# Nearest-neighbour upsampling: one SBUF tile, output rows of up to 64 KB, 16 DMAs instead of 24

## Chip, cores and metric

The kernel runs on one core of one Trainium2 chip. The metric is device time in microseconds (us). Times are medians of several runs. The span is the time from the first to the last instruction in a profiled run; it is about 1.8 us shorter than the time.

A number called "landing" is the moment at which the last of a DMA's 16 completion writes arrives. Landings and packet durations are read from the trace's completion and packet records. Sizes of single loads, stores and rows are in binary units, as the profile gives them (a 4 MB store is 4096 KB); totals such as 83.89 MB and rates in GB/s are decimal.

## The reference

```python
x: (16, 64, 64, 64) float32, scale_factor = 2
result[:, :, i, j] = x[:, :, i // 2, j // 2]        # (16, 64, 128, 128) float32
```

Nothing is computed: 16.78 MB come in, and each value goes out four times, 67.11 MB. Together they are 83.89 MB.

## The kernel before

All of the input fits in SBUF, the on-chip memory. Eight loads of 2 MB bring it in at once, 64 input rows (16 KB) to a partition each. Then 16 stages expand 32 input rows per partition into one of two buffers, VectorE (DVE) the first 18 rows and ScalarE (ACT) the other 14, and a 4 MB store takes the buffer away. One input row becomes 1 KB of output, so a partition's piece of a store is one contiguous row of 32 KB.

```python
blocks = [64, 64, 64, 64, 64, 64, 64, 64]
K = 32
KV = 18
xpool = ctx.enter_context(tc.tile_pool(name="xin", bufs=1))
upool = ctx.enter_context(tc.tile_pool(name="uexp", bufs=2))

loaded = []
first = 0
for n, k in enumerate(blocks):
    xt = xpool.tile([P, k, W], fdt, name=f"x{n}")
    nc.sync.dma_start(out=xt[:, :, :], in_=of_block(xf, first, k))
    ...
for xt, first, k in loaded:
    for r0 in range(0, k, K):
        u = upool.tile([P, K, s, W, s], fdt, name="u")
        nc.vector.tensor_copy(out=u[:, :KV], in_=expanded(xt[:, r0 : r0 + KV, :]))
        nc.scalar.copy(out=u[:, KV:], in_=expanded(xt[:, r0 + KV : r0 + K, :]))
        nc.sync.dma_start(out=of_block(of, first, k)[:, r0 : r0 + K, :], in_=u[:, :, :, :, :])
```

`begin_before_barrier` (cut here) moves the first load ahead of the start-up barrier. The change leaves it doing the same.

## Time and profile before

The time is 199.88 us (median of 6 runs, 199.73 to 200.25), the span 198.0 us.

These are lines of the page of the kernel before. The DMA row gives the mean busy share of the 16 DMA engines in tenths, for 40 equal slices of the span; the row below it gives what they moved.

```profile
span 198.0 us, 149 instructions
...
DMA  8999999999999999999999999999999999999995
...
DMA packets 3456, 83.89 MB, mean 424 GB/s; under 512 B 384, under 2 KB 384, under 8 KB 384
...
L83 ACT COPY u<-x 128x3584 f32<-128x3584 f32 x16 | 50.8, 3179 | 128.3 <-DMA out_dram<-u 122.5
L80 DVE COPY u<-x 128x4608 f32<-128x4608 f32 x16 | 40.9, 2560 | 139.7 <-DMA out_dram<-u 131.8
...
out_dram<-u SPq DMA_DIRECT2D x16, 4096.0 KB, 16.1
x<-in_x_dram SPq DMA_DIRECT2D x8, 2048.0 KB, 22.9
```

The DMA engines are full from the second slice to the last but one. The copies take 3.2 us (ACT) and 2.6 us (DVE), and both engines idle most of the time, waiting for a store to free a buffer. The packet count splits exactly: 384 completion writes (24 DMAs on 16 engines) and 3072 data packets, one for each contiguous row (8 × 128 of 16 KB, 16 × 128 of 32 KB).

The busy time of the engines in four stretches confirms the constant pace. The columns are the stretch, its length, the busy time of DVE, ACT and POOL with instruction counts, the clock, the DMA share and GB/s.

```profile
20.00:60.00 40.00, 2.56 (x1) 3.18 (x1) 0.00 (x0) 1.00 1.02 432
60.00:100.00 40.00, 10.24 (x4) 12.71 (x4) 0.00 (x0) 1.00 1.00 433
100.00:140.00 40.00, 11.01 (x5) 13.50 (x5) 0.00 (x0) 1.00 1.00 433
140.00:180.00 40.00, 11.51 (x5) 13.98 (x5) 0.00 (x0) 1.00 1.00 433
```

The chain of waits needs more care. Its columns are start, duration and what; a DMA piece runs from issue to landing.

```profile
0.00 7.82 DMA x<-in_x_dram
...
103.70 16.06 DMA out_dram<-u
...
119.86 3.19 ACT u L83
...
123.06 16.05 DMA out_dram<-u
...
142.42 16.09 DMA out_dram<-u
...
158.60 3.19 ACT u L83
```

One could read this as a serial loop of copy (3.2 us) and store (16.1 us), with the fixed cost of a DMA on the critical path. But the chain follows only every second store, because a stage waits for the buffer of two stages ago. Two stores land within 123.06 + 16.05 − (103.70 + 16.06) = 19.35 us, 9.68 us each. A store waits 6.4 us of its 16.05 us behind the one before it. Copy and fixed cost are hidden. Only what makes the engines take longer for their bytes can matter.

### The profile page before, as it was taken

How to read it: one execution, taken by the hardware profiler on the slowest of the kernel's cores; microseconds unless marked ns; L12 is line 12 of the kernel's file. 1: busy time of each engine (PE TensorE's matmuls, PEld its weight loads, DVE VectorE, ACT ScalarE, POOL GpSimd, SP SyncE). 2: the span in 40 equal slices, each digit the busy share in tenths (PEclk: the TensorE clock that was granted, in tenths of full speed). 3: DMA queues.
4: the chain of work that ended last, by engine and by line, in shares of the span. 5: the costliest groups of instructions: out<-in, count | busy, mean ns of one | idle time of the engine just before them, and what ended most of it. 6: DMA issues, size and time to landing. Idle time of an engine off the chain costs nothing.

```text
span 198.0 us, 149 instructions
## 1 busy us (share of the span) xinstructions
DVE 40.9 (21%) x16; ACT 52.0 (26%) x17; POOL 0.2 (0%) x4
## 2 busy tenths in 40 slices
DVE  0460000000405050505050505050505050504000
ACT  2480000000415150606060606060606060605000
POOL 0000000000000000000000000000000000000000
DMA  8999999999999999999999999999999999999995
GB/s 268 434 434 434 430 427 430 424 427 424 424 424 437 444 463 430 437 430 430 424 424 424 424 437 444 457 437 430 437 430 424 424 424 424 437 437 463 437 430 232
DMA packets 3456, 83.89 MB, mean 424 GB/s; under 512 B 384, under 2 KB 384, under 8 KB 384
## 3 DMA queue, kind: packets, MB, share of 16 engines
q1 hardware_dynamic: 3456, 83.89, 99.0%
HBM read 16.78 MB, written 67.11 MB: 424 GB/s over the span
## 4 chain that ended last, share of the span: by engine, by line
DMA 77%; ACT 14%; issue 0%; ACTq 0%
DMA out_dram<-u 73%; ACT u L83 14%; DMA x<-in_x_dram 4%; ACTq L83 0%
## 5 line engine op out<-in xcount | busy, mean ns | idle before, releaser
L83 ACT COPY u<-x 128x3584 f32<-128x3584 f32 x16 | 50.8, 3179 | 128.3 <-DMA out_dram<-u 122.5
L80 DVE COPY u<-x 128x4608 f32<-128x4608 f32 x16 | 40.9, 2560 | 139.7 <-DMA out_dram<-u 131.8
L83 ACT ACT_TABLE_LOAD x1 | 1.3, 1283 | 0.8 <-PEq L106 0.8
L106 POOL MEMSET const-bfloat16-1.0<- 128x1 bf16 x1 | 0.1, 102 | 0.0
L106 POOL MEMSET const-uint8-127<- 128x1 uint8 x1 | 0.1, 102 | 0.0
L106 POOL MEMSET const-float32-0.0<- 128x1 f32 x1 | 0.1, 98 | 0.2 <-issue 0.2
L106 POOL MEMSET const-float32-1.0<- 128x1 f32 x1 | 0.1, 98 | 0.0
## 6 DMA issues: line engine op xcount, KB each, us to landing
out_dram<-u SPq DMA_DIRECT2D x16, 4096.0 KB, 16.1
x<-in_x_dram SPq DMA_DIRECT2D x8, 2048.0 KB, 22.9
```

Of the source, the lines that this page charges most:

```text
L80: nc.vector.tensor_copy(out=u[:, :KV], in_=expanded(xt[:, r0 : r0 + KV, :]))
L83: nc.scalar.copy(out=u[:, KV:], in_=expanded(xt[:, r0 + KV : r0 + K, :]))
L106: nc = _bacc.Bacc("TRN2", target_bir_lowering=False, num_devices=1)
```

## The change

The intent: fewer and longer pieces. One SBUF tile of 192 KB per partition holds the input (128 KB) and an output space (64 KB). The first half of the output leaves as before, through two halves of that space. By then half of the input is consumed, and the second half of the output leaves in four 8 MB stores whose pieces are rows of 64 KB. They alternate between the 64 KB of consumed input and the 64 KB of output space. The input comes in four loads of 4 MB; the fourth comes as four rows of 8 KB per partition. The 24 DMAs become 16.

```diff
-    blocks = [64, 64, 64, 64, 64, 64, 64, 64]
-    K = 32
-    KV = 18
+    WX = R // P * W
+    WU = 16384
+    mem_pool = ctx.enter_context(tc.tile_pool(name="mem", bufs=1))
+    mem = mem_pool.tile([P, WX + WU], fdt, name="mem")
+    M4 = R // (4 * P)
+    blocks = [(1, M4, 0), (1, M4, 2), (1, M4, 3), (4, M4 // 4, 1)]   # pieces, input rows in each, place
+    WB = M4 * W
 ... (the loads: one for each block, into mem[:, slot * WB : (slot + 1) * WB])
+    def store(part, r0, k, at):
+        xp, first, m = part
+        kv = k * 9 // 16
+        u = mem[:, at : at + k * s * W * s].rearrange(
+            "p (k a w b) -> p k a w b", k=k, a=s, w=W
+        )
+        nc.vector.tensor_copy(out=u[:, :kv], in_=expanded(xp[:, r0 : r0 + kv, :]))
+        nc.scalar.copy(out=u[:, kv:], in_=expanded(xp[:, r0 + kv : r0 + k, :]))
+        dst = of[first : first + P * m, :].rearrange("(p m) w -> p m w", p=P)
+        nc.sync.dma_start(out=dst[:, r0 : r0 + k, :], in_=u)
+    small = [(q, r0) for n in (0, 3) for q in parts[n] for r0 in range(0, q[2], 32)]
+    large = [(q, r0) for n in (1, 2) for q in parts[n] for r0 in range(0, q[2], 64)]
+    for n, (q, r0) in enumerate(small):
+        store(q, r0, 32, WX + n % 2 * (WU // 2))
+    for n, (q, r0) in enumerate(large):
+        store(q, r0, 64, (0, WX)[n % 2])
```

(The old loops, and a generalised `begin_before_barrier` that still moves one load, are cut.)

More of the change, by code (lines that the diff above doesn't have):

```diff
@@ L6 @@
 from concourse._compat import with_exitstack
+EARLY = 1
 def begin_before_barrier(nc):
@@ L15, in begin_before_barrier @@
     sp = mybir.EngineType.SP
-    load = next(i for i in body.instructions if i.engine == sp)
-    assert isinstance(load, mybir.InstDMACopy), type(load)
-    assert not (load.sync_info and load.sync_info.on_wait)
-    body.instructions = [i for i in body.instructions if i is not load]
+    loads = [i for i in body.instructions if i.engine == sp][:EARLY]
+    for load in loads:
+        assert isinstance(load, mybir.InstDMACopy), type(load)
+        assert not (load.sync_info and load.sync_info.on_wait)
+    names = [i.name for i in loads]
+    body.instructions = [i for i in body.instructions if i.name not in names]
     kept = list(main.instructions)
@@ L25, in begin_before_barrier @@
     )
-    kept.insert(at, load)
+    kept[at:at] = loads
     main.instructions = kept
@@ L44 @@
     fdt = x.dtype
-    blocks = [64, 64, 64, 64, 64, 64, 64, 64]
-    K = 32
-    assert P * sum(blocks) == R
-    KV = 18
+    WX = R // P * W
[5 more added lines that the diff above has]
+    WB = M4 * W
+    assert M4 * P * 4 == R and 2 * WB == WU
     xf = x.rearrange("b c h w -> (b c h) w")
     of = out.rearrange("b c (h hd) w -> (b c h) (hd w)", hd=s)
-    def of_block(rows, first, k):
-        return rows[first : first + P * k, :].rearrange("(p k) w -> p k w", p=P)
-    xpool = ctx.enter_context(tc.tile_pool(name="xin", bufs=1))
-    upool = ctx.enter_context(tc.tile_pool(name="uexp", bufs=2))
-    loaded = []
-    first = 0
-    for n, k in enumerate(blocks):
-        xt = xpool.tile([P, k, W], fdt, name=f"x{n}")
-        nc.sync.dma_start(out=xt[:, :, :], in_=of_block(xf, first, k))
-        loaded.append((xt, first, k))
-        first += P * k
+    parts = []
+    for n, (j, m, slot) in enumerate(blocks):
+        first = n * P * M4
+        xt = mem[:, slot * WB : (slot + 1) * WB].rearrange(
+            "p (j m w) -> p j m w", j=j, m=m
+        )
+        nc.sync.dma_start(
+            out=xt.rearrange("p j m w -> p j (m w)"),
+            in_=xf[first : first + P * M4, :].rearrange(
+                "(j p m) w -> p j (m w)", j=j, p=P
+            ),
+        )
+        parts.append([(xt[:, jj], first + jj * P * m, m) for jj in range(j)])
     def expanded(rows):
@@ L75, in expanded @@
         )
-    for xt, first, k in loaded:
-        for r0 in range(0, k, K):
-            u = upool.tile([P, K, s, W, s], fdt, name="u")
-            nc.vector.tensor_copy(
-                out=u[:, :KV], in_=expanded(xt[:, r0 : r0 + KV, :])
-            )
-            nc.scalar.copy(
-                out=u[:, KV:], in_=expanded(xt[:, r0 + KV : r0 + K, :])
-            )
-            nc.sync.dma_start(
-                out=of_block(of, first, k)[:, r0 : r0 + K, :],
-                in_=u[:, :, :, :, :],
-            )
+    def store(part, r0, k, at):
[3 more added lines that the diff above has]
+            "p (k a w b) -> p k a w b", k=k, a=s, w=W
+        )
+        nc.vector.tensor_copy(out=u[:, :kv], in_=expanded(xp[:, r0 : r0 + kv, :]))
[8 more added lines that the diff above has]
+        store(q, r0, 64, (0, WX)[n % 2])
 _INS = ['x', 'scale_factor']
```

## The prediction

> **What bounds the kernel now.** The DMA engines: 83.89 MB in a span of 198.0 us. The page's row of forty slices shows the DMA share full from the second slice to the last but one; the windows from 20 to 180 us show 432 to 433 GB/s each. The chain of waits gives ACT 14%, but misleads: stores take 16.05 us from issue to landing and land 9.68 us apart, so each is issued 6.4 us before its predecessor lands, and the 3.2 us copy is hidden. About 1.0 us passes before the first packet, 0.8 us after the last landing; 1.86 us lie between span and reported time.
>
> **What the change does.** Bytes and the DVE:ACT split (9:7) stay. 24 DMAs become 16: 8 loads of 2 MB become 3 of 4 MB in 32 KB rows and one of 4 MB in 8 KB rows; 16 stores of 4 MB become 8 the same and 4 of 8 MB in 64 KB rows. Data rows fall from 3072 to 2432 (192 to 152 per engine), completion writes from 384 to 256.
>
> **Cost of what is removed.** The tempting sum is 8 DMAs at the ~2 us fixed cost that the Trainium skill ("DMA: Bandwidth & Descriptors", Anatomy of one DMA) gives for a single DMA: 16 us. The trace denies it here: with another DMA queued, that latency is covered. What remains is a gap per row. Per engine, loads land 4.892 us apart for 8 rows of 16 KB, stores 9.680 us for 8 rows of 32 KB. If both directions run at one rate, that is 27.4 GB/s per engine and 0.104 us of overhead per DMA of 8 rows, some 12 ns per row. Estimate from this: three loads save 0.1 us each, the 8 KB-row load gives back 0.2, four large stores save 0.1 each: 0.5 us in all; 0.2 us if part of the loads' lower rate is due to direction. All of it is on the critical path.
>
> **What it adds, off the path.** A large store needs 5.1 us of DVE beside 6.4 us of ACT (twice today's). At today's pace, loads finish at 42 us and small stores land until 119.6. The first large store, over consumed input, is ready at 110, before the last small store streams. The second needs both small buffers free (119.6) and is ready at 126, while the first streams until 139; the others have 13 us of margin. The first copy waits for 4 MB (12.7 us instead of 7.8). The queue should never run dry.
>
> **Predicted: 199.4 us, 80% range 199.0 to 199.95.** Faster by over 2%: 1%; within 2%: 96%; slower by over 2%: 3%.
>
> **Right if:** DMA share full throughout; 4 MB stores still 9.68 us apart, large ones 19.26 rather than 19.36; 2432 data and 256 completion packets; DVE and ACT busy within 1 us; no gap.
>
> **Wrong if:** 64 KB rows are split in two packets (3200 instead of 2688; gain near 0.1 us); or the output pitch of 128 KB between partitions (64 KB before) slows HBM writes: the same page (Latency and other measured facts) reports 207 GB/s at a 512 KiB pitch against 214 at full rate; no run shows it yet; large stores over 19.5 us apart would. Or the start and the turn from loads to stores, which cost about 1 us and 0.25 us over the steady pace, change with the row size.

## The result, and the profile after

The time after is 199.50 us (median of 6, 199.42 to 199.63), against 199.88 us. The ratio is 0.998, with a 95% interval of 0.9967 to 0.9993. Ratios here are the mean time of one kernel's fast runs over that of the other's fast runs of the same rounds, so not quite the ratio of the medians. The gain is 0.1 to 0.7 us: about 0.2%, and inside the "within 2%" class. The span fell from 198.00 to 197.71 us.

Lines of the page after, to set beside those of before:

```profile
span 197.7 us, 116 instructions
...
DMA  8999999999999999999999999999999999999994
...
DMA packets 2688, 83.89 MB, mean 424 GB/s; under 512 B 256, under 2 KB 256, under 8 KB 256
...
L96 ACT COPY mem<-mem 128x3584 f32<-128x3584 f32 (+1 forms) x12 | 50.0, 4174 | 112.5 <-DMA out_dram<-mem 102.2
L95 DVE COPY mem<-mem 128x4608 f32<-128x4608 f32 (+1 forms) x12 | 40.2, 3359 | 123.1 <-DMA out_dram<-mem 110.8
...
out_dram<-mem SPq DMA_DIRECT2D x8, 4096.0 KB, 16.1
mem<-in_x_dram SPq DMA_DIRECT2D x4, 4096.0 KB, 25.8
out_dram<-mem SPq DMA_DIRECT2D x4, 32.3
```

The engines are as full as before, and the copies cost the same (50.0 against 50.8, 40.2 against 40.9 us). The 2688 packets are 256 completion writes and 2432 data packets; in the packet records 512 of them have 65,536 bytes, so a 64 KB row is one packet and is not split. An 8 MB store takes 32.3 us from issue to landing. That is no slowdown: it waits behind another 8 MB.

The stretches after, for the part where the load stage ends:

```profile
20.00:60.00 40.00, 2.56 (x1) 3.18 (x1) 0.00 (x0) 1.00 1.01 426
60.00:100.00 40.00, 15.20 (x5) 12.72 (x4) 0.00 (x0) 1.00 1.00 433
```

The stretch with the turn from loading to storing moves 426 GB/s where it moved 432. These figures are coarse where packets are large, but they point to the turn. The chain of waits after:

```profile
0.00 12.25 DMA mem<-in_x_dram
...
103.56 16.09 DMA out_dram<-mem
...
119.67 6.17 ACT mem L96
...
125.86 32.44 DMA out_dram<-mem
...
158.38 6.17 ACT mem L96
```

From 119.65 (103.56 + 16.09) to 158.30 (125.86 + 32.44) two large stores land, 38.65 us for 16 MB. Before, the same stretch, from 119.76 to 158.51, took four small stores 38.75 us. The larger ACT copy (6.17 us instead of 3.19) is hidden: the store issued at 125.86 still queues until the one ahead lands at 138.98.

The landings show where the gain came from. The five stages cover the same bytes in both kernels, and the times in us are worked out from the completion records of each profile. "Before again" is a second profile of the kernel before, from the experiments.

| stage | before | before again | after | after − before |
|---|---|---|---|---|
| first 4 MB in | 12.70 | 12.65 | 12.25 | −0.45 |
| next 8 MB in | 19.58 | 19.60 | 19.40 | −0.18 |
| last 4 MB in | 10.03 | 10.05 | 10.54 | +0.51 |
| first 32 MB out | 77.45 | 77.46 | 77.46 | +0.01 |
| last 32 MB out (64 KB rows after) | 77.43 | 77.43 | 77.25 | −0.18 |
| end, after the last landing | 0.81 | 0.81 | 0.81 | 0.00 |
| span | 198.00 | 197.99 | 197.71 | −0.29 |

The two profiles of before agree within 0.05 us in each stage, better than the times of repeated runs (0.3 us apart and more). Two profiles say little about the start and the turn, though. The two kernels of experiment 3 have the same loads as before, and there the first 4 MB took 12.78 and 12.57 us and the last 4 MB 10.46 and 10.37. Eight profiles whose first load is the same as in after spread from 12.16 to 12.41. The two store stages repeat far better (within 0.07 us wherever the stage and its rows are the same).

### The profile page after: what moved, and what is told of

Read it like the earlier page. It is cut to its first block, busy times and chain, and to the rows that moved or that the text cites. A ratio compares the mean times of both kernels' runs of the same rounds, so it can differ in the third digit from the quotient of the medians.

```text
span 197.7 us, 116 instructions
## 1 busy us (share of the span) xinstructions
DVE 40.2 (20%) x12; ACT 51.3 (26%) x13; POOL 0.2 (0%) x4
## 2 busy tenths in 40 slices
DMA packets 2688, 83.89 MB, mean 424 GB/s; under 512 B 256, under 2 KB 256, under 8 KB 256
## 3 DMA queue, kind: packets, MB, share of 16 engines
q1 hardware_dynamic: 2688, 83.89, 98.9%
## 4 chain that ended last, share of the span: by engine, by line
DMA 69%; ACT 14%; issue 0%; ACTq 0%
DMA out_dram<-mem 63%; ACT mem L96 14%; DMA mem<-in_x_dram 6%; ACTq L96 0%
## 5 line engine op out<-in xcount | busy, mean ns | idle before, releaser
L96 ACT COPY mem<-mem 128x3584 f32<-128x3584 f32 (+1 forms) x12 | 50.0, 4174 | 112.5 <-DMA out_dram<-mem 102.2
L95 DVE COPY mem<-mem 128x4608 f32<-128x4608 f32 (+1 forms) x12 | 40.2, 3359 | 123.1 <-DMA out_dram<-mem 110.8
## 6 DMA issues: line engine op xcount, KB each, us to landing
out_dram<-mem SPq DMA_DIRECT2D x4, 32.3
```

The lines of the kernel that those rows point to most:

```text
L95: nc.vector.tensor_copy(out=u[:, :kv], in_=expanded(xp[:, r0 : r0 + kv, :]))
L96: nc.scalar.copy(out=u[:, kv:], in_=expanded(xp[:, r0 + kv : r0 + k, :]))
```

## The experiments

Three theories were on the table:

- **Row theory.** Each contiguous row costs an engine a few ns beyond its bytes. The gain is proportional to the rows removed.
- **DMA theory.** Each DMA costs something, so the gain comes from 16 DMAs instead of 24.
- **For the load stage**, where a gain of 0.45 us at the start and a loss of 0.51 us at the end showed up: they follow the size of the rows, or the size of the DMAs.

In each experiment the kernel before ran in the same rounds on the same chip.

### 1. The 8 MB stores in 32 KB rows, still one DMA each

```diff
-        store(q, r0, 64, (0, WX)[n % 2])              # 64 rows of one part
+        # 32 rows of part 1 and 32 rows of part 2; their places in the output are not adjacent
+        nc.sync.dma_start(out=both[:, :, r0 : r0 + 32, :],
+                          in_=u.rearrange("p (n k) a w b -> p n k (a w b)", n=2))
```

The two expansions into one buffer take three copies instead of two; the copies stay hidden.

> The kernel after, but each 8 MB store writes two separate 32 KB rows per partition (32 rows of each of two parts), still one DMA: 64 more rows in all per 16 engines' worth of 8 rows, 16 DMAs as before. Row theory (a cost of about 6 to 9 ns per row and engine): the 8 MB stores land 19.36 us apart again instead of 19.31, the four together lose the 0.18 us that they gained, time 199.68. DMA theory (a cost per DMA): 19.31 us apart, time 199.5, because the number of DMAs is unchanged.

Measured: 199.74 us; ratio to before 0.9996 (0.9977 to 1.0015). The packets rose to 3200, as many as 64 KB rows split in two would give. Its chain of waits over the same two large stores:

```profile
103.69 16.07 DMA out_dram<-mem
...
125.97 32.50 DMA out_dram<-mem
```

From 119.76 to 158.47 these are 38.71 us, against 38.65. Over all four large stores, landings take 77.41 us: the pace of before (77.43), not of after (77.25). The DMA count did not change, so the DMA theory fails here.

### 2. The same rows, in twice as many DMAs

```diff
-        nc.sync.dma_start(out=dst[:, r0 : r0 + k, :], in_=u)
+        for h in range(0, k, 32):
+            nc.sync.dma_start(out=dst[:, r0 + h : r0 + h + 32, :], in_=u[:, h : h + 32])
```

> The kernel after, but each 8 MB store is issued as two 4 MB DMAs of 32 KB rows from the same buffer: 20 DMAs instead of 16. Row theory: pairs land 19.36 us apart as in the run with the same number of DMAs and two rows, plus 9 ns for a completion write, time 199.7. DMA theory: this one alone loses the gain, time 199.7, and the run with two rows per DMA does not. If DMAs cost near 2 us each[...], time is 207.

Measured: 200.15 us; ratio 1.0011 (0.9993 to 1.0029). The last 32 MB took 77.44 us, against 77.41 with half the DMAs: four more DMAs cost at most 0.03 us while the queue is full. The row theory had expected 199.7. The excess is not in the data stream at all: the last landing is at 197.10 us, yet the span ends at 198.16, so the end is 1.06 us instead of 0.81. The trace's records of SyncE explain it. At the end SyncE waits for the eight DMA semaphores, always in the same order, and the DMAs use them in turn. With 16, 24 or 72 DMAs the last DMA's semaphore is also the last waited for. With 20, four more waits follow it, about 62 ns each. Every run agrees: 0.81 us with 16, 24 and 72 DMAs, 1.06 with 20, 0.94 with 14 (two more waits). Part of this kernel's 200.15 us is so explained; the rest of the difference of its median is within the spread of its runs (199.92 to 200.34).

### 3. Stores in 8 KB rows, with 24 DMAs and with 72

To see a row's cost above the noise, the kernel before got rows four times shorter: 384 more rows for each engine. Once a store stays one DMA, once it is four.

```diff
+            dst = of_block(of, first, k).rearrange("p (j h i) w -> p j h i w", j=4, h=2)[:, :, h]
+            src = u.rearrange("p (j i) a w b -> p j i (a w b)", j=4)
-            nc.sync.dma_start(out=of_block(of, first, k)[:, r0 : r0 + K, :], in_=u[:, :, :, :, :])
+            nc.sync.dma_start(out=dst, in_=src)                     # b_rows8_same_dmas
+            for j in range(4):                                      # b_rows8_more_dmas
+                nc.sync.dma_start(out=dst[:, j], in_=src[:, j])
```

> The kernel before, but each 4 MB store writes four separate 8 KB rows per partition in one DMA instead of one row of 32 KB. The number of DMAs (24) stays; data rows rise by 384 per engine. Row theory: 384 times 6 to 9 ns, 2.3 to 3.5 us slower, stores land 9.83 to 9.90 us apart, time 202.2 to 203.4. DMA theory: no change, 199.9.

> The kernel before, but each 4 MB store is issued as four DMAs of 1 MB in 8 KB rows: 72 DMAs instead of 24, with the same 384 more rows per engine as the run with one DMA of four rows. Row theory: as that run plus 48 completion writes of 9 ns, 0.4 us: 202.6 to 203.8. DMA theory at the size that the gain of after suggests (0.38 us for 8 DMAs, 0.05 us each): 2.3 us slower, 202.2, while the run with one DMA stays at 199.9. At 2 us for each DMA: 296.

Measured: 203.59 us with 24 DMAs (ratio 1.0195, 1.0181 to 1.0209) and 203.17 us with 72 (1.0175, 1.0161 to 1.0189). The packet rows of the two pages, 24 DMAs first:

```profile
DMA packets 9601, 83.90 MB, mean 416 GB/s; under 512 B 384, under 2 KB 384, under 8 KB 384
```

```profile
DMA packets 10371, 83.92 MB, mean 417 GB/s; under 512 B 1152, under 2 KB 1152, under 8 KB 1152
```

Both kernels have 9216 data packets; the rest are completion writes and, by the packet records, one and three 8 KB packets of another queue, kind "instruction". Three times the DMAs made nothing slower; the kernel with more of them was even 0.4 us faster, for which no cause was sought. Against the 199.68 us of before on that chip, the shorter rows cost 3.9 and 3.5 us. The DMA theory asked for the opposite order and for no loss with 24 DMAs. The row theory has the direction right. Its size was somewhat low with 24 DMAs (2.3 to 3.5 us expected); with 72 (0.4 more expected) the time of 203.17 us lies inside its range.

The size is not one constant, though. With 24 DMAs the stores landed 9.78 to 9.80 us apart up to 141 us, 0.12 more than with 32 KB rows, which is 5 ns for each of the 24 added rows. From there they came 9.96 to 10.02 us apart, one 10.52 and the last 9.70. (The one "instruction" packet, at 185.58 us, falls into the long one.) In the mean of the 16 completion writes the pace changes earlier, from 9.80 us for the store that lands at 111 us to 9.98 for the one at 131. The kernel with 72 DMAs slows down too, from 9.81 us for each 4 MB to about 10.0 after 140 us. Why the pace falls late in both kernels stays open, and so does the part of the 3.9 and 3.5 us that it makes up: 384 rows at 5 ns would be 1.9 us.

### 4. The last load in other rows, and at another place

Three edits of the kernel after, each with 16 DMAs of the same size. They ask whether the loss at the turn comes from the 8 KB rows of the last load.

```diff
-    blocks = [(1, M4, 0), (1, M4, 2), (1, M4, 3), (4, M4 // 4, 1)]
+    blocks = [(1, M4, 0), (1, M4, 2), (1, M4, 3), (1, M4, 1)]        # a_load4_rows32
+    blocks = [(1, M4, 0), (1, M4, 2), (1, M4, 3), (2, M4 // 2, 1)]   # a_load4_rows16
-    for n, (j, m, slot) in enumerate(blocks):
+    for n in (0, 3, 1, 2):                                           # a_load4_second
```

> The kernel after, but the fourth load brings one 32 KB row per partition in place of four 8 KB rows. In the trace of after, the fourth load landed 10.54 us after the third (9.70 between the others). Row theory: 24 rows fewer per engine at 9 ns save 0.2 us, of 0.84; the turn from reading to writing keeps the other 0.6: fourth landing at 10.3. Turn theory (short rows make the turn from loads to stores longer): back to 9.95 as before the change had it, so 0.55 us saved, time 198.95 to 199.0. No output of this kernel changes its value; the output rows' pitch does, from 32 to 128 KB, for four stores.

> The kernel after, with the load in 8 KB rows issued second instead of last; nothing else moves. Row theory: the same rows, so the same time, 199.5; the load in 8 KB rows lands 9.9 us after the first wherever it stands, and the last load, of 32 KB rows, 9.95 to 10.3 after its predecessor. Turn theory: the 8 KB rows cost 0.2 us in mid-stream and the turn is short again, 9.95: 0.3 to 0.4 us faster than after, 199.1 to 199.2.

> The kernel after, but its last load brings two 16 KB rows per partition in one DMA instead of four of 8 KB; still 16 DMAs. If the cost of the turn follows the row size of the load before it (about 0.25 us of landing with 16 KB, 0.6 to 0.9 with 32 KB, 1.3 with 64 KB), the last load lands 10.05 us after the third instead of 10.54 and the time is 199.1, the fastest of all. If it follows the size of the last DMA (2 MB before, 4 MB after), it stays at 10.45 and the time at 199.45.

| kernel | last load's rows | last 4 MB in, us | time, us | ratio to before |
|---|---|---|---|---|
| after | 8 KB | 10.54 | 199.50 | 0.998 (0.9967 to 0.9993) |
| a_load4_rows32 | 32 KB | 10.57 | 199.57 | 0.9984 (0.9967 to 1.0) |
| a_load4_second | 32 KB | 10.45 | 199.47 | 0.9977 (0.9959 to 0.9995) |
| a_load4_rows16 | 16 KB | 10.80 | 199.62 | 0.9976 (0.9963 to 0.999) |
| before | 16 KB, in 2 MB DMAs | 10.03 | | |

The bet on rows lost three times. Neither longer rows nor 16 KB rows, those of before, restored the 10.03 us. With 8, 16 and 32 KB rows, a last load of 4 MB lands 10.45 to 10.80 us after the one before it. In this table only the smaller last DMA goes with the short turn. It isn't enough by itself: the kernels of experiment 3 have the loads of before, but 8 KB rows in the stores behind them, and their last 4 MB took 10.46 and 10.37 us. Whether that comes from the stores or differs from one execution to the next was not tested. One part did follow the rows: put second, the load in 8 KB rows landed 9.91 us after its predecessor instead of 9.71, which is 8 ns for each of the 24 more rows. None of these versions can be told from after by its time.

### 5. Load sizes: four 32 KB-row loads alone, two 8 MB loads, a 16 KB-row first load

```diff
-    blocks = [64, 64, 64, 64, 64, 64, 64, 64]
+    blocks = [128, 128, 128, 128]                                    # b_loads32, of the kernel before
-    blocks = [(1, M4, 0), (1, M4, 2), (1, M4, 3), (4, M4 // 4, 1)]
+    blocks = [(1, M4, 0), (1, M4, 1)]        # c_two_loads, of after, with M4 = R // (2 * P)
+    blocks = [(2, M4 // 2, 0), (1, M4, 2), ...]                      # a_load1_rows16, of after
```

> The kernel before, but with four loads of 4 MB in 32 KB rows in place of eight of 2 MB in 16 KB rows; its 16 stores are untouched. This is the load half of the change without the 8 KB rows and without the large stores. Row theory: 32 rows fewer per engine at 6 to 9 ns save 0.2 to 0.3 us, of which the 0.18 us of the landings 2 and 3 in after is part; the start repeats what after showed (4 MB landed at 12.25 us instead of 12.70), so in all 0.5 to 0.6 us, time 199.3. If the start of after was luck of one execution, 4 MB land at 12.7 again and the time is 199.65.

> The kernel after, with its four loads replaced by two of 8 MB in 64 KB rows (256 input rows of each partition in one piece); stores keep their sizes. Rows per engine fall from 152 to 112, DMAs from 16 to 14; output pitch between partitions rises from 128 to 256 KB. Row theory: 40 rows at 6 to 9 ns save 0.25 to 0.35 us and the turn, without 8 KB rows, another 0.3: 198.9. If the first packets' slow start grows with the row, less. If the pitch slows HBM writes, 4 MB stores land over 9.75 us apart.

> The kernel after, but its first load brings two 16 KB rows per partition in one DMA instead of one row of 32 KB; still 16 DMAs. Start theory (the slow first packets cost more with shorter rows): 4 MB land at 12.70 us, as before, instead of 12.25, and the time is that of before less 0.1: 199.75 to 199.9. Row theory alone: 8 rows more per engine at 6 to 9 ns, 12.32 us, time 199.55 to 199.6.

| kernel | load DMAs | first 4 MB in | loads 2 and 3 (8 MB) | last 4 MB in | all loads in | end | time, us | ratio to before |
|---|---|---|---|---|---|---|---|---|
| before | 8 | 12.70 | 19.58 | 10.03 | 42.31 | 0.81 | | |
| after | 4 | 12.25 | 19.40 | 10.54 | 42.19 | 0.81 | 199.50 | 0.998 |
| b_loads32 | 4 | 12.41 | 19.41 | 10.34 | 42.15 | 1.06 | 199.92 | 1.001 (0.9996 to 1.0024) |
| a_load1_rows16 | 4 | 12.26 | 19.43 | 10.70 | 42.39 | 0.81 | 199.74 | 0.9987 (0.9975 to 1.0) |
| c_two_loads | 2 | | | | 42.49 | 0.94 | 199.91 | 1.0009 (0.9996 to 1.0021) |

`b_loads32` is the load half of the change. It repeats its shape, an earlier first 4 MB (0.29 us), 0.17 us in mid-stream and a later last load (0.31 us): 0.16 us earlier in all. Then its 20 DMAs give 0.25 us back at the end, as in experiment 2, and the time is no better than before. The expected 199.3 us was wrong.

`a_load1_rows16` asks about the start: 16 KB rows in one 4 MB DMA land at 12.26 us, not at 12.70. So short rows alone don't make the late start, and fewer, larger load DMAs go with the early one. The row's length may still be part of it. A landing is set by the last engine alone; in the mean of the 16 completion writes the first 4 MB arrive at 12.20 to 12.25 us in the four profiles with 2 MB loads, at 11.89 to 12.02 in the eight with a first load in 32 KB rows, and here, in between, at 12.08.

`c_two_loads` was meant as the best version, with the fewest rows of all (112 per engine against 152), and was not faster. Its second load landed 20.58 us after the first, 1.27 us over the 19.31 us in which such 64 KB rows pass in its stores. The GB/s row of its page shows the dip in the ninth slice:

```profile
GB/s 423 423 423 423 423 423 423 423 311 430 423 423 423 423 423 450 450 450 443 430 423 423 423 423 423 476 450 489 476 436 423 423 423 423 423 423 423 423 423 212
```

Over the steady pace, the turn thus costs about 0.25 us with a last load of 2 MB in before (5.14 us against 4.89; 0.6 to 0.7 us in the kernels of experiment 3), 0.6 to 1.1 us with 4 MB, and 1.3 us with 8 MB. `c_two_loads` also served as a test of the output pitch, 256 KB between partitions: its small stores still land 9.68 us apart once the first has landed (77.52 us for eight, the first of them 9.76).

### 6. Two turns instead of one

```diff
+    for n, r0 in enumerate((0, 32)):
+        store(parts[0][0], r0, 32, WX + n % 2 * (WU // 2))
+    load(3)                                  # the fourth load, issued behind two stores
```

> The kernel after, with its last load issued behind the first two stores, so that the queue turns from reading to writing twice and back once; bytes, rows and DMAs are those of after. If every turn from reading to writing costs what the one in after costs over the steady pace (0.6 to 0.85 us) and the way back costs nothing, 0.6 to 0.85 us slower, 200.1 to 200.35; if the way back costs as much, 200.8 to 201.2. Row theory and DMA theory: no change, 199.5.

Measured: 199.94 us; ratio to before 0.9999 (0.9985 to 1.0012). The last landing is at 197.19 us, 0.29 us later than in after. The third load, now the one before the first turn, landed 10.62 us after its predecessor, about 0.9 over the pace. Around the second turn no such loss is found: the two stores, the load in 8 KB rows and the store after it took 39.08 us, and at their own paces they would take 38.95. So a turn does not have one fixed price: in this run most of it is paid at the first one. What the engines do there is not visible in the packets of the stores, which take their usual 1213 ns; the last load packets take longer.

### 7. The kernel before against itself

> The kernel before, once more, against itself: a second profile of it. Every theory: 199.8 in time and a ratio of 1.000. It tells how far a start and a turn repeat: in the first profile 4 MB had landed at 12.70 us and the last load landed 5.14 us after the one before it, 0.25 us over the pace of the others.

Measured: 200.03 against 200.01 us; ratio 0.9995 (0.9982 to 1.0007). Its stages stand in the table of the result. On that chip the kernel before is 0.13 us slower than in the runs of the result, so times from different chips should not be compared to 0.1 us.

## Why the prediction was right

The predicted time was 199.4 us and 199.50 was measured, inside the range.

- **The bound, and what is hidden: shown.** The queue stayed full, and the tempting 16 us for eight DMAs did not appear. The Trainium skill ("DMA: Bandwidth & Descriptors", Anatomy of one DMA) gives about 2 us of fixed cost for each DMA, in a section on DMAs issued from GpSimd; the DMAs here are issued from SyncE, and no run here has one alone. Experiment 3 shows 48 more DMAs at no cost when others are queued.
- **The gain per row of the stores: right in kind, half in size.** The prediction had four large stores saving 0.1 us each, landing 19.26 us apart. They landed 19.29 to 19.33 us apart. All seven kernels with 64 KB rows took 77.22 to 77.27 us for the last 32 MB; all five with 32 KB rows in the same place took 77.40 to 77.44. The means differ by 0.18 us, for 32 rows fewer per engine: 5.6 ns a row. The mis-sized term is the 12 ns, which was read off loads and stores together "if both directions run at one rate".
- **The loads in mid-stream: right in size.** 16 rows fewer saved 0.17 to 0.18 us, 11 ns a row if the rows alone did it. But loads 2 and 3 are also two DMAs where there were four, and no run separates the two here. The 8 KB rows gave back 0.2 us, seen alone in experiment 4 with the number of DMAs unchanged, 8 ns a row.
- **The start and the turn: named as a risk, not sized.** The start gained 0.45 us where a first load was worth 0.1, and the turn lost about as much. The whole load stage ended only 0.12 us earlier, and in the mean of the 16 completion writes not clearly earlier at all (41.91 and 41.77 us in the two profiles of before, 41.88 in after). That start and turn nearly cancelled was luck. The cause of both is open. The experiments exclude the row's length as the whole cause of the start, and the last load's rows as the cause of the turn. Both go with the size or number of the load DMAs, which these runs did not separate, and experiment 3 shows that these don't settle the turn alone.
- **What it adds off the path: shown.** The first large store was issued at 109.76 us (110 predicted), the second at 125.86 (126), and no gap appeared at the stores.
- **The feared output pitch: not seen.** The Trainium skill ("DMA: Bandwidth & Descriptors", Latency and other measured facts) reports a loss at a 512 KiB pitch. At 64, 128 and 256 KB here, 32 KB rows kept 9.68 us a store.

In sum, the prediction had 0.5 us from rows; the runs show 0.18 us from rows in the large stores, 0.18 in mid-stream from rows and perhaps fewer DMAs, and a start and a turn that nearly cancel. The measured span fell by 0.29 us.

## What to carry to other kernels

When the DMA queue never runs dry, do not multiply the number of DMAs saved by the fixed cost of one: read the distance between landings, and price a change by the contiguous rows that each engine no longer handles. With rows already at 16 to 32 KB little is left to win: the bytes alone need 192.7 us of the 198.0, an estimate at the 435.3 GB/s that a store keeps without its rows (worked out below). What is left then sits at the start, at the turn from loading to storing and at the end, where even the number of DMAs decides how many waits follow the last landing.

## What the Trainium skill lacked or had wrong

- "DMA: Bandwidth & Descriptors", Where 436 GB/s comes from, gives 435.2 GB/s. The runs agree: a store's 9.680 us, less 8 rows of 5.6 ns, is 435.3 GB/s for 4 MB, an estimate. "HBM Reference", Specifications (TRN2), has about 358 GB/s as one core's share and about 425 GB/s for a core that streams alone; this core held 433 GB/s in the steady stretches.
- "DMA: Bandwidth & Descriptors" speaks of a fixed overhead for each packet only to explain why small ones are slow, and gives no measured cost for a row of many KB. Here it is about 5 to 6 ns per row and engine in stores (8 to 64 KB, until the late slowdown below) and 8 ns in loads (8 against 32 KB; 11 ns for 16 against 32 KB, with fewer DMAs as well).
- That page's fixed cost of about 2 us stands in a section on DMAs issued from GpSimd, and it could say that queued DMAs hide such a cost, as they did here for DMAs issued from SyncE: 72 DMAs instead of 24 were 0.4 us faster, not 96 us slower.
- No page read has the cost of the turn from loading to storing: 0.25 us after a last load of 2 MB (0.6 to 0.7 with stores in 8 KB rows behind it), 0.6 to 1.1 us after 4 MB, 1.3 us after 8 MB, and in the one run with two turns most of it at the first.
- No page read has the closing waits: about 62 ns for each DMA semaphore waited for after the last landing, 0.81 us with none and 1.06 us with four.
- No page read explains why stores in 8 KB rows went from about 9.8 to 10.0 us for each 4 MB in the later part of the run, after 110 to 141 us, in both kernels that have them.
